# The lower half of the last gate's modulation as partial sums on VectorE in the gate pairs of the convolution branch

## The chip, the core and the metric

The kernel runs on one core of a Trainium2 chip. A core has TensorE (PE, matrix products; its weight loads are PEld in the profile), VectorE (DVE), ScalarE (ACT), GpSimd (POOL) and SyncE (SP, which here only issues transfers), each with its own queue of instructions, taken in order. The metric is the device time of one execution in microseconds (us), the median of several runs.

## The reference

One layer of a diffusion backbone over 128 context tokens and 512 latent tokens with 1024 channels: a SwiGLU feed-forward half-step, a mixer (an mLSTM and a gated convolution, joined and projected), and a second feed-forward half-step. Each of the three parts is modulated by vectors made from a conditioning vector: nine vectors of 1024 channels, for context and latent tokens apart.

```python
mod = jax.nn.silu(cond) @ w_mod + b_mod
sh1, sc1, g1, shm, scm, gm, sh2, sc2, g2 = jnp.split(mod, N_MOD, axis=-1)
...
h = modulate(rmsnorm(x, norm_g[2]), sh2, sc2)
x = x + 0.5 * g2[:, None, :] * swiglu(h, ffn2_w1, ffn2_w2)
```

The change concerns `g2`, the gate of the last half-step: 1024 columns of `w_mod` for two conditioning vectors. Its lower half is its first 512 channels: 2 MB of fp32 weights, four loads of 512 KB.

## The kernel before

All 640 tokens stay on the chip with channels on the partitions, in two halves of 320 columns. Every fp32 weight tile is split into a high part `wh` (a cast on ScalarE) and a low part `wl` (a subtraction on VectorE, line 79), and every product is three matmuls of 320 columns (lines 245 to 247). The large products are done in pairs of output blocks by a scheme of seven products (`pair_steps`): VectorE forms four sums of weight quarters (`ws`, line 218), TensorE does the products A11, S1, S2, A12, S3, S4, A22 with the activations H11, HT1, HT2, H21, HT3, H22, HT4 of the names in the profile, and ScalarE and VectorE combine them in PSUM. A pair is 84 matmuls. Two combinations matter here. The product S3 ends in PSUM tile `c`; VectorE reads it there (line 294) before the last product, A22, writes the same tile. And what the pair after needs is cast four products ahead.

Weights come through SP's queue into a ring of five buffers of 512 KB (`wr`). An element of the program lists its loads (`raws`); a load goes out when the buffer five loads earlier is done with. The program is a list of elements written out by hand; an element's `fill` is a list of small steps that are put between its products.

The modulation vectors are computed in three ways. `mod_half` (and `mod_mid`, which puts it into a head) lets TensorE multiply the weights by the two conditioning columns `cm`: a unit for each of four loads, 16 matmuls of 32 columns by 256 (line 574) in all, then a copy of two halves out of PSUM (`rows_`, line 581, on VectorE and ScalarE), four turns by TensorE (line 586) and a reduction and addition on VectorE (lines 591, 593). `mod_dve` lets VectorE form the partial sums: for each load two channels for each of the two vectors (lines 694 and 696), accumulated in two tiles of 512 columns; when all four loads are in, TensorE sums over the partitions by matmuls with ones (`red`, line 705), ScalarE copies the result (708), TensorE turns it (`turn`, 713), and VectorE adds the bias (`fin`, 721). `with_units` spreads such units evenly over a list of elements.

Around the change the program runs so: the output product of the mLSTM (with units of `mod_dve`), the convolution's pairs, the four pairs of its gate (`gsc_pair`, 1042 to 1092 us), its output product and the merged output product (with units of `mod_dve` into two tiles of the activations' pool), a last element in halves, and then the head of the second feed-forward (`head_el`): the first two pairs of blocks as plain products, while VectorE and ScalarE normalise, modulate and split the second half of the tokens (`right_chain`) and form the sums T1 to T4 of the activations for the pairs that follow. The head's `mid` elements are the four units of `mod_mid(G2, 0)`: two ahead of its products, two between the halves. The gate is used after the head, where `half_gate(G2)` halves it and the second matrix's products are added.

Of the kernel before, what the change touches and what calls it, by code (L numbers as in the profile page):

```python
# [14 lines left out]
KT = 8  # L15
# [29 lines left out]
def mixer_step(ctx: ExitStack, tc: tile.TileContext, x_prompt, x_sample, state_C, state_n, state_m,  # L45
# [93 lines left out]
    def raw(n):  # L139
        load_more()  # L140
        return rtile[n]
# [40 lines left out]
    def step(fn):  # L182
        return element([], [], fn)

    def weave(main, extra):
        n, m = len(main), len(extra)
        e = 0
        out = []
        for i, el in enumerate(main):
            el = dict(el, fill=[])  # L190
            out.append(el)
            while e < m and e * n < (i + 1) * m:
                if extra[e]["raws"] or out[-1] is not el:
                    out.append(extra[e])
                else:
                    el["fill"].append(extra[e])
                e += 1
        return out + extra[e:]
# [106 lines left out]
    def pair_el(load1, load2, ev, e1=None, spare_v=False):  # L305
        po = pair_ops(e1=e1)

        def emit():
            nf = len(fill)
            for i, _ in enumerate(pair_steps(ORDER, ev, spare_v)):  # L310
                relax(7 - i if i else 9)
                drain(nf - nf * (i + 1) // 7)
        return dict(element([load1, load2], [po[name] for name in ORDER], emit), pair=True)
# [350 lines left out]
    def mod_mid(ch, half):  # L664
        us, fs = mod_half(ch, half)
        els = []
        for i, (load, emit) in enumerate(us):
            def go(w, emit=emit, last=(i == 3)):
                emit(w)
                if last:  # L670
                    soon.append(fs[0])
                    lazy.extend(fs[1:])
            els.append(dict(element([load], [], go), calm=True))
        return els
# [56 lines left out]
    def with_units(main, units, spare=0):  # L731

        out = []
        n, m = len(main) - spare, len(units)
        e = 0
        post = []
        for i, el in enumerate(main):
            el = dict(el, raws=list(el["raws"]), fill=list(el.get("fill", ())))
            now, post = post[:1], post[1:]
            while e < m and e * n < (i + 1) * m:  # L740
                load, fns, more = units[e]
                at_ = len(el["raws"])
                el["raws"].append(load)
                for j, fn in enumerate(fns):
                    def go(fn=fn, at_=at_, el=el, last=(j == len(fns) - 1)):
                        fn(raw(el["base"] + at_))
                        if last:
                            rdone.add(el["base"] + at_)
                            load_more()
                    el["fill"].append(step(go))  # L750
                post += [step(f) for f in more]
                e += 1
            el["fill"] += now
            out.append(el)
        assert e == m
        return out + [step(lambda: lazy.extend(p["emit"] for p in post))]

    def gain(n, sc, k0=0, nk=KT):
        def f():
# [118 lines left out]
    def right_chain(n, sh):  # L878

        def all_of(*fs):  # L880
            def f():
                for x in fs:
                    x()
            return f

        def right(k):
            if k < 4:
                HB.setdefault("12", [None] * 4)[k] = hl = hpair("T4")
                split(N[1, k], *hl)
            else:  # L890
                put("22", k - 4, N[1, k])

        def rows(k0, k1):

            for k in range(k0, k1):
                if k < KT:
                    scale_x(1, k, N["rb", 1])
                if 1 <= k <= KT:
                    modulate(1, k - 1, n, sh)
                if k >= 2:  # L900
                    right(k - 2)

        def t1(k):
            N["T", k] = utile()
            V.tensor_sub(N["T", k], N[1, k], N[0, k])

        def t2(k):
            V.tensor_sub(N["T", k], N[1, k + 4], N["T", k])

        def t3_(k):  # L910
            V.tensor_sub(N[1, k], N[1, k + 4], N[1, k])

        def t4(k):
            V.tensor_sub(N["T", k], N[0, k + 4], N["T", k])
        ks = range(4)
        work = [lambda k=k: t1(k) for k in ks] + [lambda k=k: put("T1", k, N["T", k]) for k in ks]
        work += [lambda k=k: t3_(k) for k in ks] + [lambda k=k: put("T3", k, N[1, k]) for k in ks]
        work += [lambda k=k: t2(k) for k in ks] + [lambda k=k: put("T2", k, N["T", k]) for k in ks]
        work += [lambda k=k: t4(k) for k in ks]
        last = [lambda k=k: put("T4", k, N["T", k]) for k in ks]  # L920
        if n in (1, 2):

            N["later"] = [all_of(*p) for p in zip(work[24:28:2], work[25:28:2])] + [all_of(*p) for p in zip(last[::2], last[1::2])]
            work, last = work[:8] + work[16:24] + work[8:16], []
        def fetch():

            if n == 2:
                A.activation(tp.tile([P, 3], F32, name="rstd", bufs=2)[:, 0:1], eps, AF.Silu)

        chain = [stat_fn(1), all_of(rows_fn(1), fetch, lambda: rows(0, 6)), lambda: rows(6, 9), lambda: rows(9, 10)]  # L930
        return chain + last, work
# [19 lines left out]
    def ffn(w1, w2, g, lists, head_of, n_head, e1=None):  # L951

        head, els, f0 = [], [], 0
        for size in GROUPS:
            U = {}
            grp = []
            for j in range(size):
                sa = {}

                def ev(mi, h, src, sa=sa, j=j, U=U):  # L960
                    if mi == 0:
                        sa[h] = t3()
                        A.activation(sa[h], src, AF.Silu)
                    else:
                        V.tensor_mul(sa[h], src, sa[h])

                        def put_u():
                            U[j, h] = hl = (PO["u"].tile([P, HT], F32R, name="Uh", bufs=12),
                                            PO["u"].tile([P, HT], F32R, name="Ul", bufs=12))
                            split(sa[h], *hl)  # L970
                        lazy.append(put_u)
                p = (w_load(w1, 0, KT, (f0 + j) * P, 2 * DFF), w_load(w1, 0, KT, DFF + (f0 + j) * P, 2 * DFF), ev)
                if f0 + j < n_head:
                    head.extend(blocks_of(p))
                else:
                    grp.append(pair_el(*p, e1 if f0 == 0 else None))
            acts = lambda k, h, U=U: U[k, h]
            ld = lambda m, f0=f0, size=size: w_load(w2, f0 * P, size, m * P, D)
            last = f0 + size == NFF
            w2s = [plain_el(ld(m), size, acts, lambda h, ps, m=m, last=last: add_x(m, h, ps, g, last))  # L980
                   for m in range(KT if not last else 2)]
            w2s[0] = dict(w2s[0], calm=False)
            if last:
                w2s.append(halves_el([ld(m) for m in range(2, KT)], size, acts,
                                     lambda m, h, ps: add_x(m + 2, h, ps, g, True), lists))
            els.append((grp, w2s))
            f0 += size
        return head_of(head), els
# [851 lines left out]
    def gsc_pair(m):  # L1840
        def ev(mi, h, src):
            if h == 0:
                GS[m + mi] = xp.tile([P, T], F32, name="x", bufs=KT)
            A.activation(GS[m + mi][:, hsl(h)], src, AF.Sigmoid, bias=bias(GSC_OFF + (m + mi) * P))
        return z_load(GSC_OFF + m * P), z_load(GSC_OFF + (m + 1) * P), ev
# [3 lines left out]
    def t_in(m):  # L1849
        def f():  # L1850
            for h in range(2):
                TL[m, h] = t = t3()
                G.dma_start(t, td[m][:, hsl(h)])
        return f
# [47 lines left out]
    for m in range(0, KT, 2):  # L1902
        if m:
            prog += [pair_el(*cx_pair(m), G), pair_el(*cx_pair(m + 1), G)]
        prog.append(pair_el(*bg_pair(m), G, spare_v=True))
    prog += weave([pair_el(*gsc_pair(m)) for m in range(0, KT, 2)], [step(lambda: None)] * 3 + [step(t_in(0))])
    y_acts = lambda k, h: YB[k, h]
    sc = [plain_el(w_load(w_sc_out, 0, KT, m * P, D), KT, lambda k, h: PB[k, h], sc_ev(m)) for m in range(KT)]
    for m in range(KT - 1):
# [77 lines left out]
            YQ.append(y_out)  # L1987

    PO["y"] = y_queue
    head, els = ffn(ffn2_w1, ffn2_w2, G2, y_after, lambda bl: head_el(bl, *right_chain(2, SH2), mod_mid(G2, 0)), 2)  # L1990
    els[0][0][0]["fill"] = [step(f) for f in N["later"] + [lambda: None] * 6]
    prog += [head] + els[0][0] + [step(half_gate(G2))]
    for i in range(3):
# [31 lines left out]
```

## Time and profile before

| | |
|---|---|
| median of 3 runs | 1662.68 us (1661.75 to 1663.08) |
| the profiled execution | 1662.47 us |
| its span (first to last instruction) | 1660.7 us |
| granted clock of TensorE | 0.999 |
| instructions | 29312 |
| loads of modulation weights on SP, 512 KB, median to landing | 51, 3.9 us |

The profile is of one execution. Its page gives the busy time of each engine, the chain of work that ended last, and groups of instructions; the trace behind it gives every instruction with its start and duration, and, in brackets, how long the engine sat idle before it and which instruction ended that. Names of tiles are those of the program without their numbers. "L294" is line 294 of the kernel.

### The profile page before, as it was taken

What the parts mean: (1) busy time and instruction counts of PE and PEld (TensorE: products, weight loads), DVE (VectorE), ACT (ScalarE), POOL (GpSimd) and SP (SyncE); (2) the same over time, 40 slices, a digit from 0 to 9 for tenths busy, and PEclk for the clock granted to TensorE, in tenths of its full rate; (3) what the DMA queues carried; (4) which work ended last, traced back from release to release, by engine and by line L of the source; (5) the groups of instructions that cost most, each with busy time, mean ns of one, the idle gap of its engine ahead of it and who ended that gap; (6) DMA issues with size and microseconds to landing.
All of it is one profiled execution on the core that took longest, in us unless ns stands there. A gap on an engine that the chain in (4) does not pass through costs nothing.

```text
span 1660.7 us, 29312 instructions
## 1 busy us (share of the span) xinstructions
PE 1641.4 (99%) x11189; PEld 1599.5 (96%) x11189; DVE 1262.8 (76%) x2690; ACT 793.7 (48%) x1729; POOL 170.8 (10%) x258
## 2 busy tenths in 40 slices
PE   8999999999999999999999999999999999999998
PEld 5999999999999999999999999999999999999997
DVE  6867877877778878778897898789598467476576
ACT  5642542533566656555561455532275245254253
POOL 2010000000031322111121221011100000000002
PEclk9999999999999999999999999999999999999999
DMA  9454343343352434342367323367232322233222
GB/s 321 114 163 122 105 124 111 102 130 100 108 182 82 113 88 108 73 113 67 96 205 238 110 78 90 105 194 209 90 102 78 101 77 78 75 91 88 77 77 64
DMA packets 273037, 193.08 MB, mean 116 GB/s; under 512 B 7924, under 2 KB 253051, under 8 KB 272897
## 3 DMA queue, kind: packets, MB, share of 16 engines
q1 hardware_dynamic: 263280, 158.36, 33.2%
q0 software_dynamic: 9584, 32.85, 6.8%
q8 instruction: 88, 1.44, 0.4%
q14 instruction: 53, 0.43, 0.1%
q10 hardware_dynamic: 32, 0.01, 0.0%
HBM read 175.87 MB, written 15.31 MB: 115 GB/s over the span
## 4 chain that ended last, share of the span: by engine, by line
PE 89%; DVE 4%; ACT 3%; DMA 2%; issue 1%; SPq 1%; POOL 0%; ACTq 0%; DVEq 0%; POOLq 0%
PE ps L245 27%; PE ps L246 27%; PE ps L247 27%; PE ax L1583 2%; PE ax L1614 2%; DMA wr<-in_ffn_w_dram 1%; PE ax L1586 1%; DVE wl L79 1%; PE ax L1560 1%; ACT Uh L852 1%; ACT wh L75 0%; SPq L552 0%; DVE x L937 0%; DMA wl<-in_x_sample_dram 0%; DVE Uh L844 0%
## 5 line engine op out<-in xcount | busy, mean ns | idle before, releaser
L79 DVE TENSOR_TENSOR wl<-wr,wh 128x512 fp32r<-128x512 f32 (+1 forms) x405 | 264.8, 668 | 80.5 <-ACT wh L75 77.4
L75 ACT CAST wh<-wr 128x512 fp32r<-128x512 f32 (+1 forms) x407 | 236.9, 593 | 157.6 <-PE ps L246 133.8
L79 DVE TENSOR_TENSOR wl<-ws,wh 128x512 fp32r<-128x512 f32 x292 | 206.0, 706 | 42.2 <-ACT wh L75 41.5
L75 ACT CAST wh<-ws 128x512 fp32r<-128x512 f32 x292 | 178.1, 619 | 103.5 <-DVE ws L218 64.6
L245 PE MATMUL ps<-Uh,wh 128*128 128x320 f32 x704 | 218.8, 311 | 0.0
L246 PE MATMUL ps<-Ul,wh 128*128 128x320 f32 x704 | 217.2, 308 | 0.0
L247 PE MATMUL ps<-Uh,wl 128*128 128x320 f32 x704 | 217.1, 308 | 0.0
L937 DVE SCALAR_TENSOR_TENSOR x<-ps,modT,x 128x128 f32<-128x128 f32 (+2 forms) x216 | 82.7, 433 | 113.9 <-PE ps L247 113.8
L245 PEld LDWEIGHTS ps<-Uh,wh 128*128 128x128 f32 x704 | 132.1, 188 | 1.2 <-issue 0.8
L246 PEld LDWEIGHTS ps<-Ul,wh 128*128 128x128 f32 x704 | 132.2, 188 | 0.2 <-DVE Ul L79 0.2
L247 PEld LDWEIGHTS ps<-Uh,wl 128*128 128x128 f32 x704 | 132.1, 188 | 0.0
L245 PE MATMUL ps<-HT4h,wh 128*128 128x320 f32 x376 | 118.6, 315 | 1.3 <-DVE t L294 1.3
L245 PE MATMUL ps<-H11h,wh 128*128 128x320 f32 x376 | 118.8, 316 | 0.5 <-ACT H11h L75 0.5
L245 PE MATMUL ps<-H21h,wh 128*128 128x320 f32 x376 | 117.7, 313 | 0.0
L246 PE MATMUL ps<-H11l,wh 128*128 128x320 f32 x376 | 116.5, 310 | 0.3
L246 PE MATMUL ps<-HT4l,wh 128*128 128x320 f32 x376 | 116.3, 309 | 0.1
L247 PE MATMUL ps<-H21h,wl 128*128 128x320 f32 x376 | 116.3, 309 | 0.0
L247 PE MATMUL ps<-HT4h,wl 128*128 128x320 f32 x376 | 116.2, 309 | 0.0
L247 PE MATMUL ps<-H11h,wl 128*128 128x320 f32 x376 | 116.2, 309 | 0.0
L246 PE MATMUL ps<-H21l,wh 128*128 128x320 f32 x376 | 116.1, 309 | 0.0
L245 PE MATMUL ps<-H22h,wh 128*128 128x320 f32 x344 | 107.6, 313 | 0.0
L246 PE MATMUL ps<-H22l,wh 128*128 128x320 f32 x344 | 106.6, 310 | 0.4
(440 smaller groups left out, 4489.1 us busy)
## 6 DMA issues: line engine op xcount, KB each, us to landing
wr<-in_ffn_w_dram SPq DMA_DIRECT2D x86, 512.0 KB, 3.9
wr<-in_w_in_dram SPq DMA_DIRECT2D x72, 512.0 KB, 3.9
wr<-in_w_mod_dram SPq DMA_DIRECT2D x51, 512.0 KB, 3.9
wr<-in_ffn_w_dram SPq DMA_DIRECT2D x48, 384.0 KB, 3.5
early<-in_w_mod_dram SPq DMA_DIRECT2D x13, 512.0 KB, 8.7
wr<-in_ffn_w_dram SPq DMA_DIRECT2D x20, 256.0 KB, 3.2
mg<-in_w_mod_dram POOLq DMA_DIRECT2D x8, 512.0 KB, 5.4
wr<-in_w_ml_out_dram SPq DMA_DIRECT2D x8, 512.0 KB, 4.4
```

Source lines behind the costliest of these rows:

```text
L75: A.copy(hi, raw)
L79: V.tensor_sub(lo, raw, f32(hi))
L245: PE.matmul(ps, hi[:, ws], ah, start=start, stop=False, skip_group_check=True)
L246: PE.matmul(ps, hi[:, ws], al, start=False, stop=False, skip_group_check=True)
L247: PE.matmul(ps, lo[:, ws], ah, start=False, stop=stop, skip_group_check=True)
L852: A.activation(t[:, a:b], t[:, a:b], AF.Identity, scale=sc_, bias=bi_)
L937: V.scalar_tensor_tensor(X[m][:, o + a:o + b], ps[:, a:b], modT[:, g, m, cd:cd + 1], X[m][:, o + a:o + b], op0=OP.mult, op1=OP.add)
L1560: PE.matmul(p[:, :P], S["k", dt][:, sl], S["q", dt][:, sl], start=(dt == 0), stop=(dt == 1))
L1583: PE.matmul(p2[:, :DH + 1], S["q", dt][:, sl], S["C"][d][:, dt, :], start=(dt == 0), stop=(dt == 1))
L1586: PE.matmul(p1[:, :DH + 1], S["p", ch][:, d, :], PO["vt"][:, ch, :], start=True, stop=True)
L1614: PE.matmul(p[:, :DH + 1], kw[:, dt * P:(dt + 1) * P], PO["vt"][:, ch, :], start=True, stop=True)
```

## The change

The lower half of `G2` is computed by `mod_dve` instead of `mod_mid`. A new function `placed` puts its four units, by a list, on the gate's pairs: units 0 and 1 on the first pair, unit 2 on the second, unit 3 on the third; the closing steps (`red`, `turn`, `fin`) come at set places in the fourth. The accumulators are two tiles of the pool `x` (`m_wide`), whose eight buffers also take the gate's results. Three empty steps in the fourth pair's `fill` set the places of the closing steps. The head loses its `mid` elements.

```diff
+    def placed(main, units, where, posts):
+        out = [dict(el, raws=list(el["raws"]), fill=list(el.get("fill", ()))) for el in main]
+        for (load, fns, more), i in zip(units, where):
+            el = out[i]
+            at_ = len(el["raws"])
+            el["raws"].append(load)
+            for fn in fns:
+                def go(fn=fn, at_=at_, el=el, last=(fn is fns[-1])):
+                    fn(raw(el["base"] + at_))
+                    if last:
+                        rdone.add(el["base"] + at_)
+                        load_more()
+                el["fill"].append(step(go))
+        for i, j in zip(posts, range(3)):
+            out[i[0]]["fill"].insert(i[1], step(more[j]))
+        return out
...
-    prog += weave([pair_el(*gsc_pair(m)) for m in range(0, KT, 2)], [step(lambda: None)] * 3 + [step(t_in(0))])
+    gsc = weave([pair_el(*gsc_pair(m)) for m in range(0, KT, 2)], [step(lambda: None)] * 3 + [step(t_in(0))])
+    gsc[-1]["fill"] = [step(lambda: None)] * 2 + gsc[-1]["fill"] + [step(lambda: None)]
+    prog += placed(gsc, mod_dve(G2, (0,), m_wide), (0, 0, 1, 2), ((3, 2), (3, 4), (3, 5)))
...
-    head, els = ffn(ffn2_w1, ffn2_w2, G2, y_after, lambda bl: head_el(bl, *right_chain(2, SH2), mod_mid(G2, 0)), 2)
+    head, els = ffn(ffn2_w1, ffn2_w2, G2, y_after, lambda bl: head_el(bl, *right_chain(2, SH2)), 2)
```

VectorE's queue in the first gate pair, from the low part of the weights' sum S4 (first row) to the addition that reads PSUM tile `c` (last row), before:

```order
L79 TENSOR_TENSOR wl<-ws,wh 128x512
L79 TENSOR_TENSOR wl<-wr,wh 128x512
L218 TENSOR_TENSOR ws<-wr 128x512
L79 TENSOR_TENSOR wl<-wr,wh 128x512
L218 TENSOR_TENSOR ws<-ws,wr 128x512
L79 TENSOR_TENSOR wl<-ws,wh 128x512
L294 TENSOR_TENSOR t_12934<-ps,t_12874 128x320
```

The same stretch after the change:

```order
L79 TENSOR_TENSOR wl<-ws,wh 128x512
L694 TENSOR_SCALAR x<-wr,cm 128x512
L79 TENSOR_TENSOR wl<-wr,wh 128x512
L696 SCALAR_TENSOR_TENSOR x<-wr,cm,x 128x512
L218 TENSOR_TENSOR ws<-wr 128x512
L79 TENSOR_TENSOR wl<-wr,wh 128x512
L694 TENSOR_SCALAR x<-wr,cm 128x512
L696 SCALAR_TENSOR_TENSOR x<-wr,cm,x 128x512
L218 TENSOR_TENSOR ws<-ws,wr 128x512
L79 TENSOR_TENSOR wl<-ws,wh 128x512
L294 TENSOR_TENSOR t_12942<-ps,t_12874 128x320
```

Four partial sums, those of unit 0, stand ahead of line 294's addition; the four of unit 1 and the first of unit 2 stand between it and the same addition of the second pair, three of unit 2 and one of unit 3 between that and the third pair's.

ScalarE's queue in the head, where the second half's last splits (`H22h`) end and the casts of the sums T1 begin (`HT1h`), before:

```order
L75 CAST H22h<-Uh 128x320
L963 ACTIVATE t_15055<-ps 128x320
L75 CAST wh<-wr 128x512 x2
L581 COPY t_15081<-ax 128x256
L75 CAST HT1h<-Ul 128x320
```

And after the change, where line 963 has become 982:

```order
L75 CAST H22h<-Uh 128x320
L982 ACTIVATE t_15068<-ps 128x320
L75 CAST wh<-wr 128x512 x2
L75 CAST HT1h<-Ul 128x320
L75 CAST HT1h<-Uh 128x320
```

The copy of line 581 is gone, on VectorE's queue as well. Further on, in the first pair behind the head, the split of one SwiGLU result (`Uh` and `Ul`) stands some ten rows later on both engines than before, behind the casts and splits of the sums T4 and still ahead of line 294's addition.

SP's queue around the four gate pairs (`in_w_in` are the mixer's weights, two tiles for a pair, `in_w_sc_out` those of the convolution's output), before:

```order
L202 DMA wr<-in_w_in_dram 128x8x128 x28
L202 DMA wr<-in_w_sc_out_dram 128x8x128
L545 DMA wr<-in_w_mod_dram 128x2x512 x2
L202 DMA wr<-in_w_sc_out_dram 128x8x128
L545 DMA wr<-in_w_mod_dram 128x2x512
```

And after:

```order
L202 DMA wr<-in_w_in_dram 128x8x128 x22
L545 DMA wr<-in_w_mod_dram 128x2x512 x2
L202 DMA wr<-in_w_in_dram 128x8x128 x2
L545 DMA wr<-in_w_mod_dram 128x2x512
L202 DMA wr<-in_w_in_dram 128x8x128 x2
L545 DMA wr<-in_w_mod_dram 128x2x512
L202 DMA wr<-in_w_in_dram 128x8x128 x2
L202 DMA wr<-in_w_sc_out_dram 128x8x128
```

Four loads of modulation weights stand between those of the gate's pairs; the second weight tile of the second pair now takes the buffer that the first tile of the first pair leaves, where before it took an older one.

## The prediction

> **What bounds the kernel now.** I read the busy line of the page first, then the chain that ended last, then stretches of the span, then single rows of each engine's timeline. In the page's lines an engine's name is followed by its busy time and share:
>
> ```profile
> PE 1641.4 (99%) x11189; PEld 1599.5 (96%) x11189; DVE 1262.8 (76%) x2690; ACT 793.7 (48%) x1729; POOL 170.8 (10%) x258
> PE 89%; DVE 4%; ACT 3%; DMA 2%; issue 1%; SPq 1%; POOL 0%; ACTq 0%; DVEq 0%; POOLq 0%
> ```
>
> TensorE (PE) is busy for 99% and carries 89% of the chain; VectorE (DVE) at 76% seems to have room. Both are averages. The change takes from one stage, the last head, and gives to another, the four pairs of the convolution branch's gate, so I look at these two. The columns are the stretch, its length, then the busy time of PE, PEld, DVE, ACT and POOL:
>
> ```profile
> 1048.00:1060.00 12.00, 12.00 (x84) 12.00 (x83) 9.17 (x17) 8.65 (x17) 1.10 (x2) 1.00 0.45 119
> 1210.00:1220.00 10.00, 10.00 (x75) 9.99 (x72) 8.27 (x22) 9.73 (x23) 0.00 (x0) 1.00 0.92 261
> ```
>
> In the first gate pair VectorE has 9.17 of 12 us filled. In the head ScalarE (ACT) has 9.73 of 10 and VectorE 8.27: TensorE is full there, but not alone in it.
>
> **What TensorE loses and gains.** Rows are start, duration, engine, operation. The first seven are of the head and its first pair; the last six are a column sum (L705) and its turn (L713) of the same make as the added ones, from the mLSTM output's stage.
>
> ```profile
> 1208.77 0.31 PE L247 MATMUL ps<-HT4h,wl 128*128 128x320 f32 x1
> 1209.01 1.07 PE L574 MATMUL ax<-wr,cm 128*32 128x256 f32 x16
> 1210.26 0.31 PE L246 MATMUL ps<-H11l,wh 128*128 128x320 f32 x1
> ...
> 1246.25 0.31 PE L247 MATMUL ps<-HT2h,wl 128*128 128x320 f32 x1
> 1246.40 0.60 PE L586 MATMUL ax<-ident,t 128*128 128x128 f32 x4
> 1246.98 0.31 PE L246 MATMUL ps<-H21l,wh 128*128 128x320 f32 x1
> ...
> 895.75 0.31 PE L247 MATMUL ps<-Bh,wl 128*128 128x320 f32 x1
> 895.99 0.64 PE L705 MATMUL ax<-x,ones 128*32 128x256 f32 x8
> 896.81 0.31 PE L246 MATMUL ps<-Bl,wh 128*128 128x320 f32 x1
> ...
> 903.56 0.31 PE L247 MATMUL ps<-Bh,wl 128*128 128x320 f32 x1
> 903.71 0.38 PE L713 MATMUL ax<-ident,t 128*128 128x128 f32 x2
> 904.08 0.31 PE L246 MATMUL ps<-Bl,wh 128*128 128x320 f32 x1
> ```
>
> Ordinary matmuls start 0.147 us apart (84 of them make a pair of 12.33 us). Two units of the modulation push the matmul after next from 0.29 to 1.49 us: 1.20 for two units, 2.40 for the four. The four turns cost 0.73 - 0.29 = 0.44. **Removed: 2.84 us.** The column sum costs 1.06 - 0.29 = 0.77, its two turns 0.52 - 0.29 = 0.23. **Added: 1.00 us**, in the last gate pair; both wait for operands finished about a product earlier, and TensorE has no spare time there to hide them.
>
> **How much of the 2.84 us reaches the end.** In the head VectorE and ScalarE make the operands that TensorE consumes. These rows follow that chain up to TensorE's one long wait in this half of the span:
>
> ```profile
> 1225.66 0.49 DVE L79 TENSOR_TENSOR H22l<-Ul,H22h 128x320 fp32r<-128x320 f32 x1 [0.56 <-ACT H22h L75]
> 1226.21 0.41 PE L246 MATMUL ps<-H22l,wh 128*128 128x320 f32 x1
> ...
> 1229.49 0.42 DVE L581 COPY t<-ax 128x256 f32<-128x256 f32 x1
> 1229.94 0.37 ACT L581 COPY t<-ax 128x256 f32<-128x256 f32 x1 [1.18 <-DVE t L581]
> 1230.70 0.49 DVE L79 TENSOR_TENSOR HT1l<-Ul,HT1h 128x320 fp32r<-128x320 f32 x1 [0.80 <-ACT HT1h L75]
> ...
> 1246.97 0.45 ACT L75 CAST HT4h<-Ul 128x320 fp32r<-128x320 f32 x1
> 1248.59 0.48 DVE L79 TENSOR_TENSOR HT4l<-Ul,HT4h 128x320 fp32r<-128x320 f32 x1
> 1251.40 0.18 DVE L591 TENSOR_REDUCE modT<-ax 128x8 f32<-128x32 f32 x1
> 1251.70 0.68 DVE L218 TENSOR_TENSOR ws<-ws,wr 128x512 f32<-128x512 f32 x1
> 1252.90 0.48 DVE L294 TENSOR_TENSOR t<-ps,t 128x320 f32<-128x320 f32 x1
> 1253.53 0.39 PE L245 MATMUL ps<-HT4h,wh 128*128 128x320 f32 x1 [1.25 <-DVE t L294]
> ```
>
> The split that TensorE multiplies at 1226.21 ended at 1226.15. What makes it hangs on ScalarE's and VectorE's own queues, and ScalarE is 9.73 of 10 us full: TensorE arriving 2.40 us earlier waits there. Of the four units' time I count nothing (bounds 0 and 2.40; the operand's row puts it at 0).
>
> Behind that, VectorE runs without a pause from 1230.70 to the addition L294 at 1252.90, and TensorE waits 1.25 us for it. Here the change does help. ScalarE's copy L581 goes, and with it its wait of 1.18: its next casts start at 1228.76, and VectorE does its HT1 splits at 1229.49, in the place of its own L581, 1.21 earlier. Next in line is the cast HT4h at 1246.97. It follows a copy of TensorE's S2 product, which does not move, so the HT4 splits start at 1246.97 + 0.45 + about 0.05 = 1247.47 instead of 1248.59: 1.12 earlier. L591 and L593 go (1251.40 to 1251.70: 0.30). A split that stood ahead of the HT4 splits now stands behind them (0.40, since HT4's splits follow each other at that distance). L294 starts 1.12 + 0.30 - 0.40 = 1.02 earlier. TensorE, due at 1252.28 before and at 1251.84 without the turns, still waits 0.67. **The head gives 1.02 us**, not 2.84. Bounds: 0 (another wait takes over) and 4.09 (all of 2.84 and the wait of 1.25).
>
> **What VectorE gains, and who waits.** Prices first, then the first gate pair before the change, with the load into the buffer that the pair's first weights leave:
>
> ```profile
> 890.66 0.50 DVE L694 TENSOR_SCALAR x<-wr,cm 128x512 f32<-128x512 f32 x1
> 891.20 0.75 DVE L696 SCALAR_TENSOR_TENSOR x<-wr,cm,x 128x512 f32<-128x512 f32 x1
> 898.86 2.98 DVE L696 SCALAR_TENSOR_TENSOR x<-wr,cm,x 128x512 f32<-128x512 f32 x4
> ...
> 1042.31 0.31 PE L245 MATMUL ps<-H11h,wh 128*128 128x320 f32 x1
> 1045.87 0.37 SPq L202 DMA_DIRECT2D wr<-in_w_in_dram  x1
> 1047.25 0.68 DVE L79 TENSOR_TENSOR wl<-ws,wh 128x512 fp32r<-128x512 f32 x1
> 1051.12 0.69 DVE L79 TENSOR_TENSOR wl<-ws,wh 128x512 fp32r<-128x512 f32 x1 [0.78 <-ACT wh L75]
> 1051.72 0.48 DVE L294 TENSOR_TENSOR t<-ps,t 128x320 f32<-128x320 f32 x1
> 1052.88 0.31 PE L245 MATMUL ps<-HT4h,wh 128*128 128x320 f32 x1
> 1054.55 0.49 DVE L79 TENSOR_TENSOR Bl<-x,Bh 128x320 fp32r<-128x320 f32 x1 [0.98 <-ACT Bh L75]
> DMA to landing us min/median/max: 3.7/4.1/8.0
> ```
>
> A first partial sum (L694) occupies VectorE for 0.53, a further one (L696) for 0.745. Sixteen come in: 8 in pair 0, 4 each in pairs 1 and 2. VectorE takes its instructions in the order shown under the change, so what stands behind a partial sum is late by it. The instruction that matters is L294: it reads the PSUM bank that TensorE's last product of the pair (T4) writes next.
>
> *Pair 0.* Four partial sums (2 x 0.53 + 2 x 0.745 = 2.55) now stand between the split at 1047.25 and L294; the idle 0.78 ahead of 1051.12 swallows some. L294 starts at 1051.72 + 2.55 - 0.78 = 1053.49, ends at 1053.97, and TensorE follows 0.15 behind it (as 1253.53 follows 1253.38). It was due at 1052.88: **a wait of 1.24**, where none was.
>
> *Pair 1.* Up to its L294 VectorE has seven splits and four sums at 0.60, two additions at 0.40, two Bl splits at 0.41 (8.2 together), and five L696 (3.73): 11.95. It idles besides: 0.98 for the Bl cast, which hangs on ScalarE as before, and an estimated 0.7 for ScalarE's casts and a load released late. L294 starts at 1053.49 + 11.95 + 1.7 = 1067.14; TensorE goes on at 1067.77 where 1052.88 + 12.33 = 1065.21 was due. **The delay has grown to 2.56 us** in all (bounds: 1.24, pair 0's alone, and 4.3 with twice the idle time).
>
> *Pairs 2 and 3.* Pair 2's queue is 7.4 + 2.98 = 10.4 of 12.33: no further loss. Pair 3 has none.
>
> **Smaller things.** Four 512 KB loads move in SP's queue from the head to the gate pairs, where five buffers now carry 12 loads instead of 8. The tightest is the second weight tile of pair 1: issued at 1045.87, it lands at the median at 1049.97; VectorE asks for it at 1049.73, so 0.2 may be lost there, inside the bounds. The head's loads come earlier and wait for nothing. One copy on ScalarE and two tiny additions in pair 3 replace others of the head; pair 3's spare time covers them.
>
> **Sum.** +1.00 - 1.02 + 2.56 = +2.54 us on the profiled execution's 1662.47: 1665.0. That execution lies 0.21 below the median 1662.68, so I say **1665.2 us**. A measurement can tell about 0.2% from no change, here 3.3 us: the forecast is a small loss inside that. Its own range, from the bounds 1.24 and 4.3 of the gate's delay, is 1663.9 to 1667.0.
>
> **Rivals.**
>
> *VectorE's room covers the partial sums.* Speaks for it: 76% busy, and casts run four products ahead. Then +1.00 - 1.02 = 0.0: 1662.7. Against it: the slack of L294 is not four products but the 1.16 us between 1051.72 and 1052.88. Chance 0.15.
>
> *TensorE's time counts in full.* TensorE is the busiest engine, and 2.84 leaves it while 1.00 comes: -1.84, 1660.8; it needs the operands at 1226.21 to come earlier, which no row shows. Chance 0.05. The Trainium skill (Perfetto Trace Analysis, Identifying the Most-Contended Engine) says to optimize the engine of highest occupancy first, with occupancy a fair measure for VectorE; by that rule this rival would hold. The trace agrees on who is busiest (99% and 76%) and differs on who is waited for (1253.53).
>
> *A late load makes it slower than before by more than a measurement needs.* Place: the second weight tile of pair 1. VectorE's sum of it stands ahead of L294 in the same queue, so from a landing of 3.9 us on, each microsecond is one of TensorE's. At the longest landing shown, 8.0, it is +4.1: 1669.3; at 5, 1666.3. For it: the ring is fuller. Against: the median of 4.1. Chance 0.2.
>
> *The change doesn't act.* The gate's pairs don't get the partial sums: excluded by the order under the change.
>
> **How the numbers follow.** Forecast 0.6, rivals 0.15, 0.05 and 0.2. The range 1661.5 to 1668.0 leaves out most of the 0.05 below and the upper end of the late load above. Faster by over 0.2% (below 1659.4): 0.03, only if TensorE's time counted in full and the wait of 1.25 went as well. Slower by over 0.2% (above 1666.0): 0.2 of the forecast's 0.6, and most of the late load: 0.28. Within: 0.69.
>
> **What would show it.** In the gate's pairs: waits of TensorE for L294's addition of 1.2 us in pair 0 and about 1.3 more by the end of pair 1, none in pair 2. In the head: the wait before the last product of its first pair falls from 1.25 to about 0.7, and small waits for H22 appear. I am wrong if the gate's pairs show TensorE without waits, if the head gains its 2.84, or if VectorE waits for a weight tile in pair 1 by more than 0.5.

## The result and the profile after

| | before | after |
|---|---|---|
| median of 20 runs each on one chip | 1662.24 us (1661.41 to 1664.08) | 1665.38 us (1664.28 to 1666.88) |
| the profiled execution | 1662.47 us | 1664.29 us |
| its span | 1660.7 us | 1662.5 us |

The ratio is 1.0018, with a 95% interval of 1.0012 to 1.0024: a loss of about 3.1 us (2.0 to 4.0). The forecast was 1665.2, a loss of 2.5.

The page of after first, its busy line and its chain:

```profile
PE 1642.0 (99%) x11163; PEld 1599.0 (96%) x11163; DVE 1272.5 (77%) x2705; ACT 794.6 (48%) x1729; POOL 170.5 (10%) x258
...
PE 90%; DVE 4%; ACT 3%; DMA 2%; issue 1%; SPq 0%; ACTq 0%; DVEq 0%
```

The page as a whole can't tell the two kernels apart: shares move by one point. The stages can. The windows of after (stretch, length, then busy time of PE, PEld, DVE, ACT, POOL), at the first two gate pairs and in the head:

```profile
1048.00:1060.00 12.00, 11.14 (x75) 10.70 (x74) 10.83 (x20) 6.50 (x12) 0.98 (x2) 1.00 0.39 105
1060.00:1072.00 12.00, 10.87 (x73) 10.34 (x72) 10.84 (x19) 6.67 (x14) 0.13 (x1) 1.00 0.52 146
1210.00:1220.00 10.00, 9.48 (x68) 9.13 (x67) 9.31 (x24) 9.05 (x22) 1.24 (x1) 1.00 0.32 91
```

In the gate VectorE went from 9.17 to 10.83 us busy of 12, and TensorE, without a gap before, now loses about a microsecond in each window. In the head too TensorE has gaps now.

To put a size on each stage I take the starts of the same matmuls in both traces: the first of each gate pair (`H11h`), the first behind the gate (`Bh`), the first of the column sums of squares in the head (`sqacc`, written L819 before, L838 after), and the last product of the first pair behind it (`HT4h`). These are TensorE's rows of after:

```profile
1041.41 0.31 PE L245 MATMUL ps<-H11h,wh 128*128 128x320 f32 x1
...
1054.85 0.31 PE L245 MATMUL ps<-H11h,wh 128*128 128x320 f32 x1
...
1069.01 0.31 PE L245 MATMUL ps<-H11h,wh 128*128 128x320 f32 x1
...
1081.31 0.31 PE L245 MATMUL ps<-H11h,wh 128*128 128x320 f32 x1
...
1094.61 0.31 PE L245 MATMUL ps<-Bh,wh 128*128 128x320 f32 x1
...
1201.64 0.61 PE L838 MATMUL ax<-ones,sqacc 128*128 128x2 f32 x4 [0.16 <-DVE sqacc L820]
...
1255.47 0.38 PE L245 MATMUL ps<-HT4h,wh 128*128 128x320 f32 x1 [0.62 <-DVE t L294]
```

The gate's four pairs take 13.44, 14.16, 12.30 and 13.30 us, 53.20 in all. Before they took 12.33 each, from 1042.31 to 1091.64, 49.33 in all: **the gate loses 3.87**. From the sums of squares to the last product the head takes 53.83; before it was 1253.53 - 1198.66 = 54.87: **the head gains 1.04**. Between and behind, nothing moves by more than 0.2. The two stages together lose 2.83.

(The profiled executions of the kernels in this study reach the gate between 1041.4 and 1043.1 us, although nothing ahead of it was edited. Their spans carry that difference, which is why stages are compared below, beside the medians.)

### The profile page after: what moved, and what is told of

It is laid out like the page before. It is cut to its first block, busy times and chain, and to the rows that moved or that the text cites. A ratio compares the mean times of both kernels' runs of the same rounds, so it can differ in the third digit from the quotient of the medians.

```text
span 1662.5 us, 29274 instructions
## 1 busy us (share of the span) xinstructions
PE 1642.0 (99%) x11163; PEld 1599.0 (96%) x11163; DVE 1272.5 (77%) x2705; ACT 794.6 (48%) x1729; POOL 170.5 (10%) x258
## 4 chain that ended last, share of the span: by engine, by line
PE 90%; DVE 4%; ACT 3%; DMA 2%; issue 1%; SPq 0%; ACTq 0%; DVEq 0%
PE ps L245 27%; PE ps L246 27%; PE ps L247 27%; PE ax L1602 2%; PE ax L1633 2%; PE ax L1605 1%; DVE wl L79 1%; ACT Uh L871 1%; DMA early<-in_w_mod_dram 1%; PE ax L1579 1%; DMA wr<-in_ffn_w_dram 0%; DMA wr<-in_w_in_dram 0%; DVE ws L218 0%; PE ax L705 0%; ACT wh L75 0%
```

## The experiments

"Median" is the difference to the runs of before on the same chip, with the interval of the ratio turned into us; "gate" and "head" are the stages just defined, each from the profiled execution.

| kernel | median | gate pairs | gate | head |
|---|---|---|---|---|
| before | 0 | 12.33, 12.33, 12.34, 12.33 | 49.33 | 54.87 |
| after | +3.1 (2.0 to 4.0) | 13.44, 14.16, 12.30, 13.30 | 53.20 | 53.83 |
| gate_only | +4.4 (2.5 to 5.5) | 13.46, 14.16, 12.31, 13.30 | 53.23 | 54.86 |
| head_only | -0.7 (-2.3 to 0.7) | 12.30, 12.31, 12.31, 12.30 | 49.22 | 53.82 |
| half_units | +0.4 (-1.2 to 1.7) | 12.33, 12.33, 12.34, 12.33 | 49.33 | 54.86 |
| no_post | -1.0 (-2.7 to 0.3) | 12.34, 12.33, 12.33, 12.34 | 49.34 | 53.80 |
| one_load | +1.9 (0.2 to 3.2) | 13.20, 13.15, 12.33, 13.30 | 51.98 | 53.82 |
| no_second | +1.5 (0.3 to 3.3) | 13.24, 13.15, 12.31, 13.29 | 51.99 | 53.83 |
| act_copy | +2.1 (0.5 to 3.7) | 12.30, 14.18, 12.33, 13.30 | 52.11 | 53.83 |
| copy_pool | +1.4 (0.0 to 2.8) | 12.31, 13.72, 12.60, 13.30 | 51.93 | 53.81 |
| spread | +1.6 (0.3 to 3.2) | 12.33, 12.34, 13.21, 13.90 | 51.78 | 53.83 |
| late_post | -0.6 (-2.0 to 1.0) | 12.30, 12.31, 12.31, 12.30 | 49.22 | 53.81 |
| copy_first | -1.2 (-2.5 to 0.3) | 12.33, 12.33, 12.33, 12.34 | 49.33 | 53.45 |
| copy_late | -1.8 (-2.8 to 0.2) | 12.33, 12.34, 12.33, 12.33 | 49.33 | 53.01 |

### The two halves of the change apart: gate_only and head_only

In gate_only the head gets its units back, in the kernel after:

```diff
-    ... lambda bl: head_el(bl, *right_chain(2, SH2)), 2)
+    ... lambda bl: head_el(bl, *right_chain(2, SH2), mod_mid(G2, 0)), 2)
```

> The lower half is made twice: in the gate's pairs as after the change, and in the head as before it. Theory (VectorE's queue ahead of the addition L294 costs TensorE 2.9 us in the gate's first two pairs, the column sum and its turns 1.0): 3.9 us above before, with the same two waits for L294 in the gate's pairs and the head's wait of 1.25 for L294 back. Rival (the loss comes from something that the head lacks since the change): at most 1 us above before.

In head_only the same line of before loses them, and a `memset` fills the gate's lower half.

> Before, with the last gate's lower half left out altogether (zeros stand in its place), so only the removal from the head acts. Theory (of TensorE's 2.84 us in the head only 1.0 reaches the end): 1.0 us below before, the wait ahead of the last product of the head's first pair 0.6, small waits for H22. Rival (TensorE's time counts in full): 2.8 us below before.

The stages come apart cleanly: gate_only has after's gate (53.23) and before's head (54.86), head_only has before's gate and after's head (53.82). TensorE's waits by what ended them (total, times, longest) between 1030 and 1270 us, in gate_only:

```profile
PE ps L245 <- DVE t L294: 3.2, 3, 1.2
PE ax L838 <- DVE sqacc L820: 0.2, 1, 0.2
```

and in head_only:

```profile
PE ax L820 <- DVE sqacc L802: 0.7, 2, 0.5
PE ps L245 <- DVE t L294: 0.6, 1, 0.6
```

All three waits of gate_only on the first line are for the addition L294: two in the gate, and the old 1.2 in the head. In head_only that one falls to 0.6, and TensorE waits half a microsecond longer than gate_only for the sums of squares (`sqacc`, 0.7 against 0.2). TensorE's 2.84 us are gone from the head, and 1.05 arrives: the rival that counts TensorE's time in full falls.

### Where the head's microsecond is made: half_units and no_post

half_units takes half of TensorE's modulation matmuls out of before's head and leaves everything else:

```diff
+                    if ch == G2 and i % 2:
+                        continue
```

> Before, with every second unit in the head issuing no matmuls (8 of the 16 L574 go, 1.20 us of TensorE; their part of the sum is left out); copies, turns and loads stay. Theory (TensorE's time there is covered by its wait for the H22 operands): within 0.2 us of before, and waits for H22 in the place of the matmuls. Rival (TensorE's time counts): 1.2 us below before.

no_post does the opposite: all 16 matmuls of the program stay (32 in the trace, which has two instructions for each: x16 is two units), what follows them goes, and zeros stand in the place of the result:

```diff
-                if last:
+                if last and ch != G2:
                     soon.append(fs[0])
                     lazy.extend(fs[1:])
```

> Before, with all four units' matmuls and loads kept, but without what follows them: the copies L581, the turns L586 and L591/L593 (their results are left out, zeros stand in their place). Theory (the head's gain is made by these alone): 1.0 us below before, as much as head_only, with the wait for L294 in the head's first pair at 0.6. Rival (the gain comes from the units' matmuls or loads): at most 0.4 us below before, the turns' own time.

In half_units the head takes 54.86: only a hundredth of a microsecond of what was taken out comes through. That is 0.88 us by its trace, less than the 1.20 expected: where before had 1.49 from the last matmul ahead of two units to the second one behind them (1208.77 to 1210.26), half_units has 1.05 (1208.81 to 1209.86), 0.44 less at each of the two places. Its rows show where the time went, TensorE at the operands `H22`:

```profile
1224.22 0.31 PE L245 MATMUL ps<-H22h,wh 128*128 128x320 f32 x1
...
1225.18 0.41 PE L246 MATMUL ps<-H22l,wh 128*128 128x320 f32 x1
...
1225.71 0.41 PE L245 MATMUL ps<-H22h,wh 128*128 128x320 f32 x1
...
1226.24 0.42 PE L246 MATMUL ps<-H22l,wh 128*128 128x320 f32 x1
```

TensorE begins this product at 1224.22 instead of 1224.95, stops three times in it (rows over 0.4 long are first matmuls behind a pause), and reaches the same last split at 1226.24, where before had 1226.21. In no_post the head takes 53.80, as in head_only, with every unit's matmul still there. So the whole gain of the head is made by the copies, turns and reductions behind the units, which held up VectorE and ScalarE, and none by TensorE's units.

### Queue or loads in the gate: one_load and no_second

In both, units lose their load and their partial sums read the accumulator in the place of a weight tile, so that VectorE's queue stays as it is. one_load does it with three of the four units, no_second with the second alone:

```diff
-                                w_ = w[:, 512 * k + j * n:512 * k + j * n + n]
+                                w_ = acc if w is None else w[:, 512 * k + j * n:512 * k + j * n + n]
...
+            if fns is units[1][1]:
+                el["fill"] += [step(lambda fn=fn: fn(None)) for fn in fns]
+                continue
             el["raws"].append(load)
```

> After, with only the first of the four 512 KB loads kept: the partial sums of the other three units read their own accumulator in the place of a weight tile (the lower half's values are thereby others). Theory (VectorE's queue makes the gate's loss): TensorE still waits for L294 by about 1.0 in pair 0, and at least 2 us above before are left; only the late second tile of pair 2 (0.92 ahead of its sum) goes, so 0.4 to 1.1 us below after. Rival (late loads make the loss): level with before, no wait for L294 in pair 0.

> After, without the load of the second unit alone: its four partial sums read their accumulator (the lower half's values are thereby others), the loads of the other three units stay. After has pair 1 of the gate at 14.16 us, one_load at 13.15. Theory (the second weight tile of pair 2 is late because its ring buffer is held by the second unit until the last of its partial sums, queued behind the splits): pair 1 at 13.2 as with three loads gone, pair 0 at 13.2 to 13.5. Rival (any fuller ring or more traffic makes it late): pair 1 at 13.7 or more.

In one_load neither theory had it whole. With three of the loads gone the first pair still takes 13.20 and the second 13.15, 1.69 above before: VectorE's queue alone. But 1.25 of after's loss in these pairs (0.24 and 1.01) goes with the loads, more than I had given them. no_second came out by its theory: 1.21 of the 1.25 goes when one load goes. Taking out any load also moves the later ones to a buffer that comes free earlier, so by itself no_second shows only that the ring is too full; which buffer it is stands in after's rows, first VectorE's and then SP's, where a row with x2 reaches from the first issue's start to the second's end:

```profile
1058.25 1.53 DVE L696 SCALAR_TENSOR_TENSOR x<-wr,cm,x 128x512 f32<-128x512 f32 x2
1059.70 0.69 DVE L218 TENSOR_TENSOR ws<-wr,ws 128x512 f32<-128x512 f32 x1
...
1062.52 0.75 DVE L696 SCALAR_TENSOR_TENSOR x<-wr,cm,x 128x512 f32<-128x512 f32 x1
1064.19 0.69 DVE L218 TENSOR_TENSOR ws<-wr 128x512 f32<-128x512 f32 x1 [0.92 <-DMA wr<-in_w_in_dram]
...
1066.61 0.48 DVE L294 TENSOR_TENSOR t<-ps,t 128x320 f32<-128x320 f32 x1
```

```profile
1051.35 8.82 SPq L202 DMA_DIRECT2D wr<-in_w_in_dram  x2
```

The second of these issues runs from about 1059.80 (1051.35 + 8.82 less its own 0.37). It is the third pair's second weight tile, and it goes into the buffer that the second unit holds, whose last two partial sums end at 1059.78. These stand in the queue behind splits and sums, so the transfer starts late, and VectorE waits for it at 1064.19, ahead of the addition L294 on which TensorE hangs. In no_second the same sum starts on time:

```profile
1062.62 0.75 DVE L696 SCALAR_TENSOR_TENSOR x<-wr,cm,x 128x512 f32<-128x512 f32 x1
1063.29 0.69 DVE L218 TENSOR_TENSOR ws<-wr 128x512 f32<-128x512 f32 x1
```

### Taking work off VectorE's queue: act_copy, copy_pool and spread

act_copy lets ScalarE copy tile `c` out in the gate's pairs, so that L294's place is taken by an addition (L292) that TensorE does not wait for:

```diff
-    gsc = weave([pair_el(*gsc_pair(m)) for m in range(0, KT, 2)], ...
+    gsc = weave([pair_el(*gsc_pair(m), spare_v=True) for m in range(0, KT, 2)], ...
```

> After, with ScalarE copying the bank out ahead of the addition in the gate's pairs, so that L294 no longer reads the bank that TensorE's last product writes (ScalarE gets one copy more per pair, about 0.4). If only L294's place in the queue costs: the waits of the gate go, 2.8 us below after, level with before. If the whole queue is late (splits and Bl casts too, behind the partial sums): the wait of pair 0 goes, but it comes back in pair 1 ahead of products whose weights or ScalarE copies are late, and only 0.8 to 1.5 us are won.

copy_pool does that in pairs 0 and 1 alone and gives two of their four sums of weight quarters to GpSimd (`G if m < 4 else None, spare_v=m < 4`).

> After, with the gate's pairs 0 and 1 relieved twice: ScalarE copies the bank out as in act_copy, and GpSimd makes two of the four sums of each pair (2 x 0.6 us of VectorE per pair). Theory (VectorE's queue, 11 of 12 us full, is what makes the loss): the waits of pairs 0 and 1 shrink to under 1 us together, 2.0 us below after, 1 us above before. Rival (loads or the ring): as late as after.

spread does both in all four pairs and places the units at (0, 1, 2, 2).

> After, with the units in pairs 0, 1, 2 and 2 in the place of 0, 0, 1 and 2, and with ScalarE's copy and GpSimd's two sums in all four pairs of the gate. Theory: TensorE has no wait left in the gate; what stays is the column sum and its turns, +1.0, against the head's 1.0: within 0.5 us of before, 2.6 below after. If TensorE's time counted in full, 1.8 us below before.

act_copy came out as its second case. Pair 0 is free (12.30), and in pair 1 the whole delay is back (14.18), at another place. TensorE's waits there:

```profile
PE ps L245 <- ACT ps L273: 1.0, 1, 1.0
PE ax L838 <- DVE sqacc L820: 1.0, 2, 0.5
PE ps L245 <- DVE t L294: 0.6, 1, 0.6
```

The first line is in the gate (the other two are in the head). TensorE waits there at 1058.56 for ScalarE's copy L273, which stands behind a cast of a sum that VectorE made late. VectorE's rows, then ScalarE's:

```profile
1056.10 0.75 DVE L696 SCALAR_TENSOR_TENSOR x<-wr,cm,x 128x512 f32<-128x512 f32 x1
1056.77 0.69 DVE L218 TENSOR_TENSOR ws<-wr 128x512 f32<-128x512 f32 x1
```

```profile
1057.56 0.62 ACT L75 CAST wh<-ws 128x512 fp32r<-128x512 f32 x1 [1.02 <-PE ps L247]
1058.09 0.42 ACT L273 COPY ps<-ps 128x320 f32<-128x320 f32 x1
```

The cast starts at 1057.56, 0.10 behind the end of the sum at 1057.46 (the trace names an older event, a product of TensorE, as its releaser). So it is VectorE's queue that is late, not the one addition, and of 2.94 us in pairs 0 and 1 only 1.12 is won. Some of that is lost again: from the gate to the sums of squares act_copy takes 107.31 us and spread 107.29, the other kernels 107.02 or 107.03.

copy_pool and spread won 1.3 and 1.4 us in the gate, not the 2 and 2.6 that I had expected; the expected price of GpSimd's help was the miss. In copy_pool these are VectorE's rows of the first pair, then GpSimd's:

```profile
1047.26 0.74 DVE L696 SCALAR_TENSOR_TENSOR x<-wr,cm,x 128x512 f32<-128x512 f32 x1
...
1048.96 1.52 DVE L694 TENSOR_SCALAR x<-wr,cm 128x512 f32<-128x512 f32 x1
1050.52 1.67 DVE L696 SCALAR_TENSOR_TENSOR x<-wr,cm,x 128x512 f32<-128x512 f32 x1
```

```profile
1048.45 3.19 POOL L218 TENSOR_TENSOR ws<-wr 128x512 f32<-128x512 f32 x2 [14.78 <-DMA wr<-in_w_in_dram]
```

In these two pairs act_copy is the same kernel without GpSimd's sums, and has these rows for the same two partial sums:

```profile
1050.18 0.48 DVE L694 TENSOR_SCALAR x<-wr,cm 128x512 f32<-128x512 f32 x1
1050.69 0.75 DVE L696 SCALAR_TENSOR_TENSOR x<-wr,cm,x 128x512 f32<-128x512 f32 x1
```

Beside GpSimd's sums they take 1.52 and 1.67: 1.96 more on VectorE's queue, against 1.2 for the two sums taken off it (2 x 0.60). In spread no wait is left in pairs 0 and 1, but pair 2, with two units, is 0.88 too long and pair 3 0.60 beyond its column sum. The one wait there that its trace names is 0.62 for ScalarE's copy L291, which stands behind a cast that ScalarE could only start once GpSimd had made its sum. VectorE is slowed beside GpSimd there too (two L696 in a row take 2.46 from 1075.84, against 1.53 in after's row at 1058.25); this was not taken further apart.

### Can the head's gain be had without the gate's loss: late_post, copy_first and copy_late

late_post leaves the units on TensorE in before's head and moves what follows them to the second pair behind it:

```diff
-                if last:
+                if last and ch == G2:
+                    PO["post"] = fs
+                elif last:
...
+    els[0][0][1]["fill"] = [step(lambda i=i: PO["post"][i]()) for i in range(3)]
```

> Before, with what follows the head's units (copies L581, turns L586, L591/L593) moved from the head and its first pair to the second pair. Theory: the first pair's wait for L294 falls from 1.25 to 0.6, but the turns' 0.44, until now beside that wait, come on TensorE's path in the second pair: 0.6 us below before. Rival (only the units' removal helps the head): level with before.

copy_first lets ScalarE copy tile `c` out in the first pair behind the head, and copy_late has both edits:

```diff
-                    grp.append(pair_el(*p, e1 if f0 == 0 else None))
+                    grp.append(pair_el(*p, e1 if f0 == 0 else None, spare_v=g == G2 and f0 + j == n_head))
```

> Before, with ScalarE copying the bank out ahead of the addition in the first pair behind the head alone, so that TensorE's last product there doesn't wait for L294. Theory (that wait of 1.25 is the one place where the head's stage is late): the wait goes, 0.9 to 1.25 us below before. Rival (ScalarE, 9 of 10 us full there, becomes late instead): level with before.

> Before, with copy_first's and late_post's edits together. Theory: the wait goes by the first, and the second only frees VectorE and ScalarE behind it: 1.2 us below before, hardly more than copy_first. If the two gains added up, 1.6.

In the head late_post gains the full 1.06 and gives 0.40 back in the second pair, where the turns now cost TensorE their time. copy_first gains 1.42 in the head: the wait of 1.25 is gone, but one of 0.32 for ScalarE's L273 comes behind it, and 0.50 is given back by the last product of the second pair. In copy_late the last product follows without a pause and no wait behind it is left:

```profile
1251.89 0.31 PE L245 MATMUL ps<-HT4h,wh 128*128 128x320 f32 x1
...
1262.44 0.60 PE L586 MATMUL ax<-ident,t 128*128 128x128 f32 x4
```

Its median is 1660.49 us, 1.8 below before, with an interval (0.9983 to 1.0001) that just reaches no change. By the stages it gains 1.86 in the head and gives back 0.33 in the second pair, where the turns stand at 1262.44. What is left, 1.53, is nearly the sum of the others' 0.66 and 0.92: the gains add up, and my theory (hardly more than copy_first) was wrong. It is the fastest kernel of the study, 4.9 us below after by the two medians, though not shown to be faster than before by the runs alone.

## Why the prediction was right, and what in it was not

**TensorE's 2.84 us in the head.** Right that only 1.02 of it reaches the end; measured 1.04 in after and 1.05 in head_only. The reason held as well: half_units shows half of the units' time at nothing, no_post the whole gain with all of it still there. The chain held row by row. These are VectorE's rows of after, whose head runs 2.98 later than before's (1201.64 against 1198.66):

```profile
1250.41 0.49 DVE L79 TENSOR_TENSOR HT4l<-Ul,HT4h 128x320 fp32r<-128x320 f32 x1 [0.38 <-ACT HT4h L75]
...
1254.84 0.49 DVE L294 TENSOR_TENSOR t<-ps,t 128x320 f32<-128x320 f32 x1
```

Less 2.98, the splits start at 1247.43 (forecast 1247.47), behind a wait for the cast HT4h as forecast, and L294 at 1251.86 (forecast 1251.88). The wait left ahead of the head's last product is 0.62 where 0.67 was forecast, and the small waits for `H22` are there:

```profile
1226.71 0.42 PE L245 MATMUL ps<-H22h,wh 128*128 128x320 f32 x1
1227.23 0.41 PE L246 MATMUL ps<-H22l,wh 128*128 128x320 f32 x1
```

**The added 1.00 in the last gate pair.** Measured 13.30 - 12.33 = 0.97. Nothing hides it.

**Pair 0.** A wait of 1.24 was forecast, and the pair is 1.11 longer. no_second (0.91) puts 0.20 of that on the second weight tile of pair 1, the 0.2 that the prediction said may be lost there. The rest is the queue. VectorE's rows with TensorE's among them:

```profile
1052.45 0.48 DVE L294 TENSOR_TENSOR t<-ps,t 128x320 f32<-128x320 f32 x1
1052.85 0.74 DVE L696 SCALAR_TENSOR_TENSOR x<-wr,cm,x 128x512 f32<-128x512 f32 x1
1052.99 0.41 PE L245 MATMUL ps<-HT4h,wh 128*128 128x320 f32 x1 [0.86 <-DVE t L294]
...
1053.51 0.69 DVE L79 TENSOR_TENSOR wl<-ws,wh 128x512 fp32r<-128x512 f32 x1
```

A further partial sum alone holds the queue for 0.66 (1052.85 to 1053.51), not 0.745, which was the price of four in a row.

**Pair 1.** Here two sizes of the sum were off, and only in part against each other. The delay by its end was forecast at 2.56 and measured at 1.11 + 1.83 = 2.94. The five further partial sums cost 3.4 instead of 3.73: three alone at 0.66 and two in a row from 1058.25 to 1059.70. And the idle time, set at 1.7, was 2.5: from one L294 to the next are 14.16 us (1052.45 to 1066.61), less 3.4 and the 8.2 of the forecast for the other instructions. Of the 1.7 only 0.7 was for casts and a load released late, and the load alone cost 1.01. The prediction looked for the late load at the second tile of pair 1, by its landing time, and gave it a rival of its own; what was late is the second tile of pair 2, by its issue, behind a buffer that the partial sums themselves hold. The mechanism (a ring of five with 12 loads) was named, the place was not. The prediction's own sign of being wrong, a wait of VectorE for a weight tile in pair 1 of more than 0.5, is there, 0.92 at 1064.19: in this term the rival of the late load was in part true. That the delay came within 0.4 of the forecast is in part luck: the queue alone cost 1.69 in the two pairs (one_load), less than the 2.56 that also held the estimated 0.7, and the late loads 1.25.

Nor is L294 the only place in pair 1. TensorE also stops twice before it, where the wait table names nothing. ScalarE's rows of after with TensorE's among them:

```profile
1057.44 0.62 ACT L75 CAST wh<-ws 128x512 fp32r<-128x512 f32 x1 [1.02 <-DVE ws L218]
1057.96 0.42 ACT L273 COPY ps<-ps 128x320 f32<-128x320 f32 x1
1058.44 0.42 PE L245 MATMUL ps<-HT2h,wh 128*128 128x320 f32 x1
...
1061.78 0.43 ACT L283 COPY ps<-ps 128x320 f32<-128x320 f32 x1
1062.26 0.41 PE L245 MATMUL ps<-HT3h,wh 128*128 128x320 f32 x1
```

Each product adds to the tile that the copy ahead of it fills, and starts 0.05 or 0.06 behind its end; the first copy stands behind a cast that waited for VectorE's sum. The two stops cost 0.18 and 0.30, the one for L294 1.37. In one_load they are 0.19, 0.30 and 0.35: of what the queue alone costs in pair 1, more than half is lost ahead of L294, where act_copy's edit does not reach.

No wait in pair 2, as said: 12.30.

**The rivals.** That VectorE's room covers the sums is refuted by one_load, which has no late load in pairs 0 and 1 and still loses 1.69 there. The prediction set 1.16 us of slack against that rival; of these L294's own 0.48 and the 0.15 behind it must come off, so 0.53 is to spare, and its sum did reckon with that. That TensorE's time counts in full is refuted by half_units and head_only. The Trainium skill (Perfetto Trace Analysis, Identifying the Most-Contended Engine) says to optimize the most-contended engine first, and judges TensorE by its rate of arithmetic and the share of its weight loads rather than by the busy share of its matmuls; it does not say that time taken there counts in full. Here TensorE led by both shares in the profile (99%, and 96% for the weight loads), and the engine that decided had 76 to 77%.

## What to carry to other kernels

A busy share alone does not say who is waited for: work given to an engine that takes its instructions in order is paid by the instructions queued behind it that have the least slack, here first an addition with 0.53 us to spare. Taking that one out of the way (act_copy) only uncovers the next. Time taken from the busiest engine counts only up to the next operand it waits for, so look for that operand's row before counting. And a load's buffer is held until the last reader in its queue is through, so work put on a slow or full queue also delays the transfer that is to follow into the same buffer.

## What the runs showed of the hardware

A VectorE instruction beside a GpSimd one that works on the same kind of tile takes far longer: L694 1.52 in copy_pool against 0.48 in act_copy, and L696 1.67 against 0.75, while GpSimd's two sums ran from 1048.45 to 1051.64. That GpSimd's sums do it is shown by the two kernels, which in these pairs differ in nothing else; by what means is not. The Trainium skill (SBUF — State Buffer, SBUF: two separate sides) says that the two engines share a pair of ports as an exclusive lock, held for a whole instruction, which a VectorE instruction needs if it has two inputs in SBUF or runs in a mode of two ports, and that the loser blocks. L696 has two inputs in SBUF, and its row agrees with that; for L694 no run shows which of the two holds, and no run tried another cause. GpSimd's 10% busy looked like free help; in these pairs it was not.
